# Scores of 64-wide heads as two float32r products over 128 rows, and weight loads issued ahead

## The chip, the cores and the metric

One core of one Trainium2 chip runs the whole program. The metric is device time in microseconds (us); of three executions of the kernel before, the median is 1943.73 us (1943.52 to 1948.55). Engines in the profile: PE is TensorE (matrix products), PEld its weight loads, DVE is VectorE, ACT is ScalarE, POOL is GpSimd, SP is SyncE, which here issues nearly all transfers.

## The reference

Two transformer blocks over 512 tokens of 1024 features in float32. The first has differential attention and a mixture of experts; the change leaves their work alone. The second has two layers, each a mixer and a convolution-gated feed-forward net. The even mixer has sparse attention, whose 128 keys per query are picked by a small index score, beside relative-position attention; the odd mixer has forgetting attention beside a sink-window attention. All their heads are 64 wide:

```python
qa, ka, va, qi, ki, wi, qb, kb, vb = _split(xn @ w_in, EVEN_SPLITS)
...
rel = jax.nn.relu(jnp.einsum('bqhd,bsd->bqhs', qib, k_idx).astype(jnp.float32))
score = jnp.einsum('bqhs,bqh->bqs', rel, wib)
_, idx = lax.top_k(score, topk)
...
logits = jnp.einsum('bqhd,bqkhd->bhqk', qb, k_sel).astype(jnp.float32) * scale            # sparse (dsa)
logits = jnp.einsum('bqhd,bshd->bhqs', qc, kc).astype(jnp.float32) * scale + bias[None]   # relative position (rel)
logits = (jnp.einsum('bqhd,bshd->bhqs', qb, k).astype(jnp.float32) * scale
          + fq[..., None] - f_cum[:, :, None, :])                                         # forgetting (forg)
logits = jnp.einsum('bnqkgd,bnskd->bnkgqs', qb, kband).astype(jnp.float32) * (dh ** -0.5) # window
p = jax.nn.softmax(logits, axis=-1).astype(v.dtype)
```

Each is masked before the softmax (the window's has a sink column beside it), and the probabilities multiply the values. `f_cum` is the cumulative log of the forget gates. Both halves of a mixer are joined and multiplied by `w_out`.

## The kernel before, in words

The residual lies feature-major (8 chunks of 128 features by 512 tokens). The program runs stage by stage; those of the change are C (even mixer, some 640 to 959 us of the profile) and E (odd mixer, some 1318 to 1565 us).

A big product is written as three products of type float32r, since a float32 number is held as a high and a low float32r part: high by high, high by low, low by high (`mm3`, L123 to L133). `load` (L114 to L118) brings raw weights into one of 3 buffers `wr`; `split` makes the high part `wh` by a cast on ACT (L110) and the low part `wl` by a subtraction on DVE (L111). `fm` makes feature-major outputs, 512 tokens wide; `tm` and `tm_cols` token-major ones.

A score is one plain float32 matmul of 64 contraction rows: block i of 128 queries against the first n = 128 (i + 1) keys, so n is 128, 256, 384 and 512 in each head (`soft_heads`, L641). There are three such sets of 8 heads: rel and dsa in C, forg in E. In forg a 65th row carries the decay: ones in `qa`, the sums in `ka` (`aug`). A score is followed by bias and minimum (L644, DVE), exponential (L645, ACT), reciprocal (L646) and scaling (L647, DVE), transposes (L656, PE), a copy (L658, ACT) and per head a group of value products (L668, PE). The index scores (L793) are 12 such products, with n of 256, 384 and 512; the window scores (L969) are 32, 8 of n = 128 and 24 of n = 256. Odd heads lie on partitions 64 to 127 of the `qk` tiles.

Work is emitted as units with a cost, and `weave` interleaves two lists of units at equal rates by those costs. The tile framework's list scheduler then fixes each engine's order. Each engine, and SP's queue, takes its instructions strictly in that order. Rope (`rot`, L370) sends four transfers of 64 KB each from a tile to the scratch tile `rsw`, all through SP's queue.

Of the kernel before, what the change touches and what calls it, by code (L numbers as in the profile page):

```python
# [4 lines left out]
F32 = mybir.dt.float32  # L5
# [11 lines left out]
BIG = 1e36  # L17
# [48 lines left out]
# per-feature vectors, packed as columns  # L66
# [15 lines left out]
class K:  # L82
# [3 lines left out]
    # ------------------------------------------------------------ helpers  # L86
# [14 lines left out]
    def split(self, raw, shape, eng=0, pool=None):  # L101
        """H, L with raw == H + L, both float32r"""
        nc = self.nc
        n = shape[1] * shape[2]
        pool, bufs = (pool, 2) if pool else (self.wp, self.nh)
        h = pool.tile([P, 1024], F32R, name="wh", tag="wh", bufs=bufs)
        l = pool.tile([P, 1024], F32R, name="wl", tag="wl", bufs=bufs)
        h = h[:, :n].rearrange("p (a b) -> p a b", a=shape[1])
        l = l[:, :n].rearrange("p (a b) -> p a b", a=shape[1])
        nc.scalar.copy(h, raw)  # L110
        (nc.gpsimd if eng else nc.vector).tensor_tensor(l, raw, h.bitcast(F32), op=OP.subtract)  # L111
        return h, l

    def load(self, src, k, n):  # L114
# [5 lines left out]
    def mm3(self, out, wh, wl, xh, xl, first, last, swap=False):  # L120
        """out += W^T x over the three products that carry float32"""
# [22 lines left out]
    # Work is emitted in units (cost, function). Units of several lists are woven, so that the tensor engine finds products to do  # L144
    # while the chain of a softmax or a norm is under way; what such a chain feeds to the tensor engine is put off by some units.
# [20 lines left out]
    def weave(a, b, tail=0):  # L166
        """one list, in which both go ahead at the same rate; the last units of b come after a"""
# [9 lines left out]
    def fm(self, w, x, done, sub=8):  # L177
        """feature-major product: done(m, psum[128 features, 512 tokens]); w [rows, cols]; x(k)->(H, L)"""
# [4 lines left out]
        raw, ps, hl = {}, {}, {}  # L183

        def unit(m, m0, per, k0, k1):
            def fn():
                if m == m0 and k0 == 0:
                    raw[0] = self.load(wv[:, :, m0 * P:(m0 + per) * P], nk, per * P)
# [14 lines left out]
        while m * P < cols:  # L203
            per = max(1, min(2048 // (nk * P), cols // P - m))
            for q in range(per):
# [6 lines left out]
    def tm(self, raws, n, x, done, nk=NK, fine=0):  # L212
        """token-major product: done(i, psum[128 tokens, n]); raws: list of (k0, k1, thunk of raw[P, k, n])"""
        ps, st, units = {}, {}, []

        def unit(k0, get, c0, c1, i):
            def fn():
                if c0 == k0 and i == 0:
                    st["raw"] = get()
# [13 lines left out]
        for k0, k1, get in raws:  # L233
            step = 1024 // n
            cuts = list(range(k0, k1, 1 if k0 < fine else step)) + [k1]
            for c0, c1 in zip(cuts, cuts[1:]):
                for i in range(NT):
                    units.append(((c1 - c0) * 3 * (n / 2400.0 + 0.003), unit(k0, get, c0, c1, i)))
# [14 lines left out]
    def sumsq(self, k):  # L253
        """self.acc: the squares of all chunks but the last; self.acc2: of the last"""
# [11 lines left out]
    def rsq(self, src, n, scale, eps=1e-6, name="rsq"):  # L266
        """(src * scale + eps) ** -0.5, [P, n]: a first guess by halving the exponent, then three steps of Newton's"""
# [33 lines left out]
    def norm_x(self, g):  # L301
        """k -> H, L of h*g, begun by the stage before or here"""
# [7 lines left out]
    def norm_lazy(self, g):  # L310
        """the same, but a chunk is made when it is first used, and the next ones with it"""
# [10 lines left out]
    def last_add(self, m, ps):  # L322
        """the last addition to a chunk of the residual in a stage"""
# [8 lines left out]
    def norm_r(self, want_b=True, now=False):  # L332
        """1 / root mean square: self.rt per token along the partitions, self.rb along the free axis"""
# [43 lines left out]
    # ------------------------------------------------------------ A: differential attention  # L377
    def stage_a(self):
# [3 lines left out]
        with tc.tile_pool(name="pa", bufs=1) as pa:  # L382
# [9 lines left out]
            # -lambda, on every partition  # L392
# [19 lines left out]
            # the queries are divided by the slopes of the heads, so that distances count 1 for all  # L412
# [157 lines left out]
    # ------------------------------------------------------------ conv gated ffn  # L570
# [57 lines left out]
    # ------------------------------------------------------------ 64-wide attention  # L628
    def soft_heads(self, pool, heads, begin):
        """units of causal attention over heads of 64; scores come negated. heads: list of dicts with q(i)->[K,128], k(n)->[K,n],  # L630
        bias(i, n)->[P,n], v(j)->[P,64], done(pv) for the second head of a pair"""
# [3 lines left out]
        def score(u, i):  # L635
# [5 lines left out]
            nc.tensor.matmul(s[:, :n], lhsT=hd["q"](i), rhs=hd["k"](n), start=True, stop=True)  # L641
# [7 lines left out]
        def turn(u, i):  # L649
# [7 lines left out]
            # block (key j, query i) lies at 3 j + i  # L657
# [17 lines left out]
        for t in range(len(us) + SOFT[1]):  # L675
            parts = [(f, us[t - d], c) for f, d, c in ((score, 0, 0.15), (turn, SOFT[0], 0.11), (value, SOFT[1], 0.3))
# [17 lines left out]
    # ------------------------------------------------------------ C: sparse + relative position attention  # L694
    def stage_c(self):
# [3 lines left out]
        self.nsb = 4  # L699
        with tc.tile_pool(name="pc", bufs=1) as pc:  # L700
            rc, rs = self.cst(pc, "ropec"), self.cst(pc, "ropes")
            tc_, ts_ = self.cst(pc, "tropec"), self.cst(pc, "tropes")
# [8 lines left out]
            def qk_tile(name, c0, n, scale, rope):  # L711
                def done(m, ps):
                    t = pc.tile([P, T], F32, name=name, tag="qk", bufs=10)
# [3 lines left out]
                    QK[name, m] = t  # L717
                return self.fm(w[:, c0:c0 + n], x, done)

            # va | ki | wi, 2 x 290 columns  # L720
# [22 lines left out]
            # layer norm and rope of the index keys, twice along the free axis so that both halves of the partitions get them  # L743
            k2 = pc.tile([P, NT, 2, 64], F32, name="k2")
            ki = pc.tile([P, T], F32, name="ki")
# [21 lines left out]
            def turn_keys():  # L767
# [3 lines left out]
                nc.scalar.copy(ki, tp)  # L771

# [3 lines left out]
            self.flush()  # L776

            # which keys each query keeps: bias 0 for kept, BIG for others
# [6 lines left out]
            def index_score(i, hh):  # L785
                def fn():
                    n = P * (i + 1)
                    if hh == 0:
                        scs[i] = pc.tile([P, T], F32, name="sc", tag="sc", bufs=2)
                    sc = scs[i]  # L790
                    b = slice(64 * (hh % 2), 64 * (hh % 2) + 64)
                    s = self.pst()
                    nc.tensor.matmul(s[:, :n], lhsT=QK["qi", hh // 2][b, i * P:(i + 1) * P], rhs=ki[b, :n], start=True,  # L793
                                     stop=True)
# [9 lines left out]
                return (0.3 * (i + 1), fn)  # L804
# [23 lines left out]
            self.emit(self.weave(index, qk_tile("qb", 1860, 512, -0.125, False) + qk_tile("kb", 2372, 512, 1.0, False)  # L828
                                 + self.tm_cols(w, 2884, 512, x, dvb)))
            yb, ya, mbs = [], [], {}  # L830

            def rel_bias(hh):
                def fn():
                    for q in range(hh + (hh > 0), min(8, hh + 2)):
                        make_bias(q)

# [9 lines left out]
            def head(kind, hh, v, begin, bias, y):  # L846
                c, b = hh // 2, slice(64 * (hh % 2), 64 * (hh % 2) + 64)
                return {"q": lambda i: QK["q" + kind, c][b, i * P:(i + 1) * P], "k": lambda n: QK["k" + kind, c][b, :n],
                        "bias": bias, "v": lambda j: v[:, j, hh * 64:hh * 64 + 64], "begin": begin, "done": self.y_out(y)}
# [5 lines left out]
            dsa = self.soft_heads(pc, [head("a", hh, va, lambda: None, lambda i, n: keep[:, ko[i]:ko[i] + n], ya)  # L855
# [4 lines left out]
    # ------------------------------------------------------------ E: forgetting attention + sink window  # L860
    def stage_e(self):
# [3 lines left out]
        self.nsb = 4  # L865
        with tc.tile_pool(name="pe", bufs=1) as pe:
            rc, rs = self.cst(pe, "ropec"), self.cst(pe, "ropes")
            wm, upto = self.cst(pe, "wmask"), self.cst(pe, "upto", tag="sb", bufs=self.nsb)
            # causal mask: 0 up to the diagonal, BIG beyond
# [9 lines left out]
            qa = pe.tile([65, 8, T], F32, name="qa")  # L879
            ka = pe.tile([65, 8, T], F32, name="ka")  # L880

            # vc | fc | vd, 2 x 324 columns; fc and the last of vc and vd come first
# [21 lines left out]
            def qk_tile(name, c0, n, scale):  # L904
                def done(m, ps):
                    t = pe.tile([P, T], F32, name=name, tag="qk", bufs=6)
                    nc.vector.scalar_tensor_tensor(t, ps, scale, self.rb, op0=OP.mult, op1=OP.mult)
                    self.rot(pe, t, t, rc, rs)
                    QD[name, m] = t
                    if name == "kd":  # L910
                        kx = QD["kx"] = pe.tile([P, T], F32, name="kx", tag="qk", bufs=6)

                        def cross():
                            nc.sync.dma_start(kx[0:64], t[64:128])
                            nc.sync.dma_start(kx[64:128], t[0:64])
                        self.after(4, cross)
                return self.fm(w[:, c0:c0 + n], x, done)

            def aug(dst, scale):
                def done(m, ps):  # L920
                    for e in range(2):
                        b = slice(64 * e, 64 * e + 64)
                        nc.vector.scalar_tensor_tensor(dst[0:64, 2 * m + e], ps[b], scale, self.rb[b], op0=OP.mult,
                                                       op1=OP.mult)
                return done
# [3 lines left out]
            # log forget gates, summed along the tokens: rows 64 of the keys  # L929
# [9 lines left out]
            def forget_sum():  # L939
# [4 lines left out]
                fr = pe.tile([8, T], F32, name="fr", tag="rsw", bufs=1)  # L944
# [685 lines left out]
```

## Time and profile before

| | us |
|---|---|
| median of three executions | 1943.73 |
| span of the profiled execution | 1942.3 |
| PE busy | 1884.1 (97%) |
| DVE busy | 1312.7 (68%) |
| ACT busy | 960.6 (49%) |
| PE's share of the chain of waits, float32 scores L641 | 3.2% |

The profiled execution is shown by its span, from the first to the last instruction; no other time of it is on the page. It lies 1.4 us below the median. Busy time is the union of an engine's instructions. The records of consecutive matmuls overlap, so the chain of waits, which gives each piece only what it adds to the end, is used for the cost of one, and not its mean duration. PEclk 1.00 is the 2.4 GHz level of TensorE's clock, 0.50 the 1.2 GHz level.

### The profile page before, as it was taken

To read this page: it belongs to the slowest core of one execution; us is meant where nothing else is said; L and a number is where in the kernel's file an instruction comes from. 1 tells how busy PE (TensorE), PEld (TensorE's weight loads), DVE (VectorE), ACT (ScalarE), POOL (GpSimd) and SP (SyncE) were. 2 spreads that over 40 slices of the span, in tenths; PEclk is the share of its full clock that TensorE was granted. 3 is DMA by queue.
4 is the path that set the end of the run, shared out by engine and by line. 5 is a ranking of instruction groups with operands and counts; after the bars stand their busy time and mean duration, and the time that the engine had idled before them with its cause. 6 is when DMAs were issued, how large, how long until landed. Compare 5 with 4: busy or idle time off the path is not lost.

```text
span 1942.3 us, 24143 instructions
## 1 busy us (share of the span) xinstructions
PE 1884.1 (97%) x8604; PEld 1452.6 (75%) x8605; DVE 1312.7 (68%) x2792; ACT 960.6 (49%) x1628; POOL 221.9 (11%) x274
## 2 busy tenths in 40 slices
PE   8999996999998899999999999999999999999997
PEld 6767585778886776665788888888666688888885
DVE  6586847999997697745577457744655577637753
ACT  5555645888885324345444234433445544324442
POOL 2000012322222202300100000012100110000001
PEclk9999997999999999999999999999999999999998
DMA  5522056999994422211232343234211133233231
GB/s 187 178 66 87 22 175 234 356 368 366 373 361 143 131 87 84 72 49 44 73 103 74 90 126 91 82 87 141 74 56 44 46 104 92 75 110 109 80 90 59
DMA packets 245680, 251.88 MB, mean 130 GB/s; under 512 B 11151, under 2 KB 172335, under 8 KB 245553
## 3 DMA queue, kind: packets, MB, share of 16 engines
q1 hardware_dynamic: 236272, 234.73, 37.9%
q0 software_dynamic: 5072, 10.00, 1.4%
q10 hardware_dynamic: 4208, 5.56, 0.8%
q8 instruction: 69, 1.13, 0.2%
q14 instruction: 59, 0.48, 0.1%
HBM read 238.19 MB, written 15.73 MB: 131 GB/s over the span
## 4 chain that ended last, share of the span: by engine, by line
PE 65%; DVE 2%; DMA 1%; issue 0%; ACT 0%; POOL 0%; DVEq 0%; ACTq 0%
PE mm L124 17%; PE mm L125 17%; PE mm L126 17%; PE s L641 3%; PE pv L668 3%; PE t L656 2%; PE mm L128 1%; PE mm L129 1%; PE mm L130 1%; PE s L969 1%; PE pv L1003 1%; DVE wl L111 1%; PE t L988 0%; PE s L793 0%; PE ss L338 0%
## 5 line engine op out<-in xcount | busy, mean ns | idle before, releaser
L110 ACT CAST wh<-wr 128x1024 fp32r<-128x1024 f32 (+5 forms) x335 | 306.7, 916 | 457.1 <-PE mm L125 329.0
L111 DVE TENSOR_TENSOR wl<-wr,wh 128x1024 fp32r<-128x1024 f32 (+4 forms) x332 | 353.6, 1069 | 214.4 <-ACT wh L110 211.7
L124 PE MATMUL mm<-xh,wh 128*128 128x512 f32 x952 | 374.3, 393 | 2.1 <-DVE h L365 1.8
L125 PE MATMUL mm<-xl,wh 128*128 128x512 f32 x952 | 372.3, 391 | 0.0
L126 PE MATMUL mm<-xh,wl 128*128 128x512 f32 x952 | 372.0, 391 | 0.0
L124 PEld LDWEIGHTS mm<-xh,wh 128*128 128x128 f32 x952 | 178.7, 188 | 45.7 <-issue 7.9
L126 PEld LDWEIGHTS mm<-xh,wl 128*128 128x128 f32 x952 | 178.8, 188 | 38.1 <-issue 1.4
L125 PEld LDWEIGHTS mm<-xl,wh 128*128 128x128 f32 x952 | 178.8, 188 | 37.4 <-issue 1.4
L111 DVE TENSOR_TENSOR wl<-wx,wh 128x1024 fp32r<-128x1024 f32 x123 | 151.6, 1250 | 12.4 <-ACT wh L110 5.8
L110 ACT CAST wh<-wx 128x1024 fp32r<-128x1024 f32 x134 | 139.5, 1050 | 28.1 <-PE mm L130 24.1
L128 PE MATMUL mm<-wh,xh 128*128 128x512 f32 (+2 forms) x352 | 132.7, 381 | 9.7 <-ACT wh L110 5.7
L125 PE MATMUL mm<-hl,wh 128*128 128x512 f32 x352 | 138.9, 395 | 0.0
L126 PE MATMUL mm<-hh,wl 128*128 128x512 f32 x352 | 138.9, 395 | 0.0
L124 PE MATMUL mm<-hh,wh 128*128 128x512 f32 x352 | 138.9, 395 | 0.0
L129 PE MATMUL mm<-wl,xh 128*128 128x512 f32 (+2 forms) x352 | 129.6, 368 | 1.4 <-DVE wl L111 1.4
L130 PE MATMUL mm<-wh,xl 128*128 128x512 f32 (+2 forms) x352 | 128.7, 366 | 0.0
L605 DVE TENSOR_TENSOR z<-mm,rb 128x512 f32<-128x512 f32 x88 | 60.3, 687 | 81.3 <-PE mm L126 81.3
L128 PE MATMUL mm<-wh,xeh 128*128 128x512 f32 x256 | 104.2, 407 | 0.8 <-ACT xeh L1262 0.8
L264 POOL TENSOR_TENSOR acc<-acc,sq 128x512 f32<-128x512 f32 x42 | 57.8, 1376 | 392.1 <-ACT sq L260 391.8
L130 PE MATMUL mm<-wh,xel 128*128 128x512 f32 x256 | 101.8, 397 | 0.0
L129 PE MATMUL mm<-wl,xeh 128*128 128x512 f32 x256 | 101.6, 397 | 0.0
L365 DVE TENSOR_TENSOR h<-mm,h 128x512 f32<-128x512 f32 x88 | 60.6, 690 | 58.3 <-PE mm L126 57.2
(386 smaller groups left out, 3324.7 us busy)
## 6 DMA issues: line engine op xcount, KB each, us to landing
wr<-in_ffn_w_up SPq DMA_DIRECT2D x88, 512.0 KB, 5.1
wx<-in_moe_w_gate SPq DMA_DIRECT2D x23, 1024.0 KB, 9.4
wx<-in_moe_w_up SPq DMA_DIRECT2D x22, 1024.0 KB, 9.0
wx<-in_moe_w_down SPq DMA_DIRECT2D x22, 1024.0 KB, 9.9
wr<-in_ffn_w_down SPq DMA_DIRECT2D x32, 704.0 KB, 4.5
wr<-in_da_w_in SPq DMA_DIRECT2D x11, 1024.0 KB, 5.1
wr<-in_even_w_in SPq DMA_DIRECT2D x11, 1024.0 KB, 5.3
wr<-in_moe_w_up SPq DMA_DIRECT2D x10, 1024.0 KB, 7.9
```

The source lines that it names most:

```text
L110: nc.scalar.copy(h, raw)
L111: (nc.gpsimd if eng else nc.vector).tensor_tensor(l, raw, h.bitcast(F32), op=OP.subtract)
L124: mm(out, lhsT=wh, rhs=xh, start=first, stop=False, skip_group_check=True)
L125: mm(out, lhsT=wh, rhs=xl, start=False, stop=False, skip_group_check=True)
L126: mm(out, lhsT=wl, rhs=xh, start=False, stop=last, skip_group_check=True)
L128: mm(out, lhsT=xh, rhs=wh, start=first, stop=False, skip_group_check=True)
L129: mm(out, lhsT=xh, rhs=wl, start=False, stop=False, skip_group_check=True)
L130: mm(out, lhsT=xl, rhs=wh, start=False, stop=last, skip_group_check=True)
L365: self.nc.vector.tensor_tensor(self.h[:, m], ps, self.h[:, m], op=OP.add)
L605: nc.vector.tensor_tensor(z[:, 2:], ps, self.rb, op=OP.mult)
L641: nc.tensor.matmul(s[:, :n], lhsT=hd["q"](i), rhs=hd["k"](n), start=True, stop=True)
L668: nc.tensor.matmul(pv[64 * e:64 * e + 64, j * P:], lhsT=heads[u]["v"](j), rhs=pt[:, 4 * j:3 * j + 4], start=j == 0, stop=j == NT - 1, skip ...
```

## The change

Scores. A query tile is cut into a high and a low float32r part (`nh` by ACT, `nl` by DVE). Transfers from SBUF to SBUF stack them for each head: `qs` holds high over low in 128 rows; `kh` holds the high part of the keys twice, `kl` their low part twice. Two float32r products over 128 rows are summed in PSUM: (high + low) queries with high keys, then with low keys. In forg the second product takes the tiles `q2` and `k2`, which also carry ones against the high and low rows of the decay.

```diff
+    def halves(self, pool, t):
+        nc = self.nc
+        h = pool.tile([P, T], F32R, name="nh", tag="nh", bufs=1)
+        l = pool.tile([P, T], F32R, name="nl", tag="nl", bufs=1)
+        nc.scalar.copy(h, t)
+        nc.vector.tensor_tensor(l, t, h.bitcast(F32), op=OP.subtract)
+        return h.bitcast(F32), l.bitcast(F32)
...
+    def q_stack(self, pool, t, tiles=None):
+        h, l = self.halves(pool, t)
+        out = []
+        for e in range(2):
+            s = tiles[e] if tiles else pool.tile([P, T], F32R, name="qs", tag="qs", bufs=self.nst)
+            self.nc.sync.dma_start(s.bitcast(F32)[self.half(e)], h[self.half(e)])
+            self.nc.sync.dma_start(s.bitcast(F32)[self.half(1 - e)], l[self.half(e)])
...
+    def k_stack(self, pool, t, low=None):
...
+            for n, name in enumerate(("kh", "kl")):
+                own = low is not None and n == 1
+                s = low[e] if own else pool.tile([P, T], F32R, name=name, tag=name, bufs=self.nst if n == 0 else self.nsl)
+                for to in (e,) if own else (e, 1 - e):
+                    self.nc.sync.dma_start(s.bitcast(F32)[self.half(to)], x[n][self.half(e)])
...
-            nc.tensor.matmul(s[:, :n], lhsT=hd["q"](i), rhs=hd["k"](n), start=True, stop=True)
+            for m, (q, k) in enumerate(hd["qk"](i, n)):
+                nc.tensor.matmul(s[:, :n], lhsT=q, rhs=k, start=m == 0, stop=m == 1)
```

Each such transfer moves 64 rows of 512, 128 KB. One pair of heads takes 12 of them in C (4 for the queries, 8 for the keys); in E a pair takes 12 and four of a single row. `prep` stacks the next pair when the scores of an odd head begin (C) or of an even one (E). The scratch `nh` is one buffer, and rope's `rsw` now uses the same; `nl` is one too. In C there are 18 such tiles to halve, in E 13. In E the 16 half-tile scalings of `aug` become 8 of whole tiles, and two cross transfers `kx` go.

```diff
+                more = lambda hh: lambda: prep("a", hh // 2 + 1) if hh % 2 and hh < 7 else None
...
-        sw = pool.tile([P, T], F32, name="rsw", tag="rsw", bufs=1)
+        sw = pool.tile([P, T], F32, name="rsw", tag="nh", bufs=1)
```

Loads. Each `fm` or `tm` registers its weight loads in the order in which they are needed, and the first use of one issues it and the next two:

```diff
+    def loaded(self, n):
+        while self.went < min(len(self.loads), n + 3):
+            self.raws[self.went] = self.loads[self.went]()
+            self.went += 1
+        return self.raws.pop(n)
```

The costs by which units are woven fall (a score's 0.15 to 0.11, an index score's 0.3 to 0.17, a window unit's 0.75 to 0.6), some buffer counts change, two rope tables share the buffers of `mb`, and the program's scratch for dynamic transfers is set to 8192.

Where instructions stand. First PE at the start of the dsa heads in C; `mm<-xh` is the last projection, `mm<-ybh` and `mm<-ybl` the output products of rel, `s` a score, `t` a transpose. Before:

```order
L128 MATMUL mm<-wh,xh_7155 128x290
L129 MATMUL mm<-wl,xh_7155 128x290
L130 MATMUL mm<-wh,xl_7157 128x290
L641 MATMUL s<-ka,qa 128x128
L641 MATMUL s<-ka,qa 128x256
L124 MATMUL mm<-ybh,wh 128x512
L125 MATMUL mm<-ybl,wh 128x512
L126 MATMUL mm<-ybh,wl 128x512
L641 MATMUL s<-ka,qa 128x384
L641 MATMUL s<-ka,qa 128x512
L124 MATMUL mm<-ybh,wh 128x512
L656 MATMUL t<-ident,sb 128x128
```

Now, at the end of 81 rows of output products (the first three of these are the last of them):

```order
L135 MATMUL mm<-ybh,wh 128x512
L136 MATMUL mm<-ybl,wh 128x512
L137 MATMUL mm<-ybh,wl 128x512
L694 MATMUL s<-kh,qs 128x128
L694 MATMUL s<-kh,qs 128x256
L135 MATMUL mm<-ybh,wh 128x512
L136 MATMUL mm<-ybl,wh 128x512
L137 MATMUL mm<-ybh,wl 128x512
L135 MATMUL mm<-ybh,wh 128x512
L136 MATMUL mm<-ybl,wh 128x512
L694 MATMUL s<-kl,qs 128x128
L694 MATMUL s<-kl,qs 128x256
```

Before, the first score follows the last projection directly and the output products stand between scores; now 81 of the 96 output products come ahead of the first score.

Second, PE at the border between two pairs of dsa heads (`pv` a value product). Before:

```order
L668 MATMUL pv<-ptall,va 64x512
L656 MATMUL t<-ident,sb 128x128 x2
L668 MATMUL pv<-ptall,va 64x384
L668 MATMUL pv<-ptall,va 64x256
L668 MATMUL pv<-ptall,va 64x128
L641 MATMUL s<-ka,qa 128x128
L656 MATMUL t<-ident,sb 128x128 x3
L641 MATMUL s<-ka,qa 128x256
L124 MATMUL mm<-ybh,wh 128x512
L656 MATMUL t<-ident,sb 128x128 x4
```

Now:

```order
L721 MATMUL pv<-ptall,va 64x128
L709 MATMUL t<-ident,sb 128x128 x4
L694 MATMUL s<-kh,qs 128x128
L694 MATMUL s<-kh,qs 128x256
L709 MATMUL t<-ident,sb 128x128 x3
L721 MATMUL pv<-ptall,va 64x512
L721 MATMUL pv<-ptall,va 64x384
L721 MATMUL pv<-ptall,va 64x256
L721 MATMUL pv<-ptall,va 64x128
L694 MATMUL s<-kl,qs 128x128
L694 MATMUL s<-kl,qs 128x256
```

The products with the high keys now stand ahead of the last values of the old pair, those with the low keys behind them, and the output product that stood there has moved.

Third, SP's queue at the same place in C. Before:

```order
L372 DMA rsw<-ka 32x512 x4
L839 DMA hk<-in_relext 128x512
L372 DMA rsw<-ka 32x512 x4
L117 DMA wr<-in_even_w_out 128x4x512
L372 DMA rsw<-ka 32x512 x8
L117 DMA wr<-in_even_w_out 128x4x512 x3
L592 DMA wr<-in_ffn_w_up 128x8x128 x22
```

Now:

```order
L128 DMA wr<-in_even_w_out 128x4x512
L385 DMA rsw<-ka 32x512 x8
L128 DMA wr<-in_even_w_out 128x4x512
L661 DMA qs<-nh 64x512
L662 DMA qs<-nl 64x512
L661 DMA qs<-nh 64x512
L662 DMA qs<-nl 64x512
L676 DMA kh<-nh 64x512 x2
L676 DMA kl<-nl 64x512 x2
L676 DMA kh<-nh 64x512 x2
L676 DMA kl<-nl 64x512 x2
```

The stacking transfers stand behind the last rope transfers and the weight loads, ahead of the first load of the feed-forward net. On all engines the order of the stages other than C and E is as before.

## Rows read from the trace of the kernel before

**Rows 1.** Page, part 1: busy us (share of the span) xinstructions.
```profile
PE 1884.1 (97%) x8604; PEld 1452.6 (75%) x8605; DVE 1312.7 (68%) x2792; ACT 960.6 (49%) x1628; POOL 221.9 (11%) x274
```

**Rows 2.** Busy time by stretch; columns: stretch, length, engines, PEclk, DMA share, GB/s.
```profile
668.00:741.00 73.00, 71.69 (x297) 53.58 (x296) 56.29 (x132) 19.18 (x26) 2.54 (x2) 1.00 0.29 90
741.00:854.00 113.00, 113.00 (x498) 73.69 (x496) 78.55 (x211) 47.74 (x117) 32.91 (x28) 1.00 0.27 79
854.00:921.00 67.00, 67.00 (x263) 36.60 (x262) 40.21 (x144) 37.15 (x106) 0.00 (x0) 1.00 0.10 31
1366.00:1469.00 103.00, 103.00 (x478) 72.01 (x477) 59.62 (x196) 49.90 (x172) 7.95 (x6) 1.00 0.20 62
1469.00:1526.00 57.00, 57.00 (x255) 36.45 (x254) 37.52 (x136) 34.05 (x99) 0.00 (x0) 1.00 0.06 19
```

**Rows 3.** Waits of PE from 668 to 921 us: total, times, longest.
```profile
PE s L793 <- DVE qi L375: 0.7, 1, 0.7
PE s L793 <- ACT rel L796: 0.6, 1, 0.6
```

**Rows 4.** Chain of waits by line: whole span, then 640 to 745 us.
```profile
by line: PE mm L124 16.9%; PE mm L125 16.6%; PE mm L126 16.6%; PE s L641 3.2%; PE pv L668 2.9%; PE t L656 1.7%; PE mm L128 1.3%; PE mm L129 1.3%; PE mm L130 1.3%; PE s L969 0.9%; PE pv L1003 0.7%; DVE wl L111 0.6%; PE t L988 0.4%; PE s L793
...
by line: PE mm L124 14.9%; PE mm L126 14.2%; PE mm L125 13.9%; PE mm L128 8.1%; PE s L793 7.8%; PE mm L130 7.4%; PE mm L129 7.3%; DMA wr<-in_even_w_in 4.9%; DVE wl L111 2.8%; PE s L641 2.6%; ACT wh L110 2.5%; issue 2.0%; PE ss L338 1.6%; DV
```

**Rows 5.** Chain, 741 to 752 us: start, length, what; heads of rel.
```profile
741.43 0.85 PE s L641 x4
742.27 0.43 PE mm L124
742.70 0.23 PE mm L125
...
743.17 1.98 PE s L641 x6
```

**Rows 6.** Chain, 858 to 866 us: heads of dsa.
```profile
858.16 0.41 PE s L641 x2
...
862.39 1.70 PE s L641 x4
```

**Rows 7.** Chain, 844 to 856 us: products 290 columns wide, then a value group.
```profile
849.29 0.13 PE mm L128
...
850.90 2.30 PE pv L668 x8
```

**Rows 8.** Lines on ACT and DVE, 640 to 960 us and 855 to 920 us, by shape.
```profile
L690 ACT CAST yah<-pv 128x512 fp32r<-128x512 f32 x4 | 2.3, 586 | 8.5 <-PE pv L668 8.5
...
L691 DVE TENSOR_TENSOR yal<-pv,yah 128x512 fp32r<-128x512 f32 x3 | 2.1, 686 | 1.9 <-ACT yah L690 1.9
```

**Rows 9.** DMA issues, 1318 to 1565 us: count, size, median us to landing.
```profile
kx<-kd SPq DMA_DIRECT2D x2, 128.0 KB, 2.3
```

**Rows 10.** Timeline of SP's queue: start, length, issue.
```profile
773.07 2.41 SPq L372 DMA_DIRECT2D rsw<-qa  x4
```

**Rows 11.** Busy time from 184 to 208 us, columns as in rows 2.
```profile
184.00:188.00 4.00, 3.53 (x23) 2.70 (x21) 0.95 (x5) 2.97 (x6) 0.00 (x0) 1.00 0.07 4
188.00:192.00 4.00, 2.76 (x14) 2.01 (x15) 3.96 (x34) 2.74 (x12) 0.00 (x0) 1.00 0.92 319
192.00:196.00 4.00, 4.00 (x15) 2.30 (x15) 3.53 (x20) 2.36 (x9) 0.00 (x0) 0.61 0.54 204
196.00:200.00 4.00, 4.00 (x9) 2.00 (x9) 1.58 (x10) 1.23 (x6) 0.00 (x0) 0.50 0.00 0
200.00:204.00 4.00, 4.00 (x13) 2.61 (x11) 1.50 (x7) 1.54 (x6) 0.00 (x0) 0.61 0.00 0
204.00:208.00 4.00, 3.90 (x22) 2.19 (x21) 3.39 (x19) 2.67 (x8) 0.00 (x0) 1.00 0.00 0
```

**Rows 12.** Waits of SP's queue, 640 to 960 us.
```profile
SPq L117 <- DVE wl L111: 95.3, 8, 28.2
```

More of the change, by code (lines that the diff above doesn't have):

```diff
@@ L112, in split, with ahead @@
         return h, l
+    def ahead(self, get):
+        self.loads.append(get)
+        return len(self.loads) - 1
+    def loaded(self, n):
[3 more added lines that the diff above has]
+        return self.raws.pop(n)
     def load(self, src, k, n):
@@ L182, in fm @@
         units = []
-        raw, ps, hl = {}, {}, {}
+        raw, ps, hl, turn = {}, {}, {}, {}
         def unit(m, m0, per, k0, k1):
@@ L187, in fn @@
                 if m == m0 and k0 == 0:
-                    raw[0] = self.load(wv[:, :, m0 * P:(m0 + per) * P], nk, per * P)
+                    raw[0] = self.loaded(turn[m0])
                 if k0 == 0:
@@ L204, in fm @@
             per = max(1, min(2048 // (nk * P), cols // P - m))
+            turn[m] = self.ahead(lambda m=m, per=per: self.load(wv[:, :, m * P:(m + per) * P], nk, per * P))
             for q in range(per):
@@ L214, in tm, with unit @@
         ps, st, units = {}, {}, []
-        def unit(k0, get, c0, c1, i):
+        def unit(k0, turn, c0, c1, i):
             def fn():
                 if c0 == k0 and i == 0:
-                    st["raw"] = get()
+                    st["raw"] = self.loaded(turn)
                 if i == 0:
@@ L233, in tm @@
         for k0, k1, get in raws:
+            turn = self.ahead(get)
             step = 1024 // n
@@ L237, in tm @@
                 for i in range(NT):
-                    units.append(((c1 - c0) * 3 * (n / 2400.0 + 0.003), unit(k0, get, c0, c1, i)))
+                    units.append(((c1 - c0) * 3 * (n / 2400.0 + 0.003), unit(k0, turn, c0, c1, i)))
         return units
@@ L626, in stage_ffn, with half @@
                 self.emit(self.fm(down[r0:r0 + HT * P], lambda k, hid=hid: hid[k], self.last_add if half else self.add_h))
+    def halves(self, pool, t):
[5 more added lines that the diff above has]
+        return h.bitcast(F32), l.bitcast(F32)
+    @staticmethod
+    def half(e):
+        return slice(64 * e, 64 * e + 64)
+    def q_stack(self, pool, t, tiles=None):
[5 more added lines that the diff above has]
+            self.nc.sync.dma_start(s.bitcast(F32)[self.half(1 - e)], l[self.half(e)])
+            out.append(s)
+        return out, h
+    def k_stack(self, pool, t, low=None):
+        x = self.halves(pool, t)
+        out = []
+        for e in range(2):
+            both = []
+            for n, name in enumerate(("kh", "kl")):
[3 more added lines that the diff above has]
+                    self.nc.sync.dma_start(s.bitcast(F32)[self.half(to)], x[n][self.half(e)])
+                both.append(s)
+            out.append(both)
+        return out
     def soft_heads(self, pool, heads, begin):
@@ L675, in soft_heads @@
         for t in range(len(us) + SOFT[1]):
-            parts = [(f, us[t - d], c) for f, d, c in ((score, 0, 0.15), (turn, SOFT[0], 0.11), (value, SOFT[1], 0.3))
+            parts = [(f, us[t - d], c) for f, d, c in ((score, 0, 0.11), (turn, SOFT[0], 0.11), (value, SOFT[1], 0.3))
                      if 0 <= t - d < len(us)]
@@ L712, in done @@
                 def done(m, ps):
-                    t = pc.tile([P, T], F32, name=name, tag="qk", bufs=10)
+                    t = pc.tile([P, T], F32, name=name, tag="qk", bufs=8)
                     nc.vector.scalar_tensor_tensor(t, ps, scale, self.rb, op0=OP.mult, op1=OP.mult)
@@ L717, in done, with prep @@
                     QK[name, m] = t
+                    if (name, m) == ("kb", 0):
+                        self.after(2, lambda: prep("b", 0))
                 return self.fm(w[:, c0:c0 + n], x, done)
+            stacks = {}
+            def prep(kind, c):
+                q, _ = self.q_stack(pc, QK.pop(("q" + kind, c)))
+                k = self.k_stack(pc, QK.pop(("k" + kind, c)))
+                for e in range(2):
+                    stacks[kind, 2 * c + e] = q[e], *k[e]
             def va_raw(part, k):
@@ L776, in stage_c @@
             self.flush()
+            qis = [pc.tile([P, 2, T], F32R, name="qis", tag="ptall", bufs=2) for _ in range(2)]
+            for c in range(2):
+                self.q_stack(pc, QK.pop(("qi", c)), [qis[c][:, e] for e in range(2)])
             keep = pc.tile([P, 1280], F32, name="keep")
@@ L790, in fn @@
                     sc = scs[i]
-                    b = slice(64 * (hh % 2), 64 * (hh % 2) + 64)
                     s = self.pst()
-                    nc.tensor.matmul(s[:, :n], lhsT=QK["qi", hh // 2][b, i * P:(i + 1) * P], rhs=ki[b, :n], start=True,
-                                     stop=True)
+                    q = qis[hh // 2][:, hh % 2, i * P:(i + 1) * P]
+                    for m, k in enumerate((kih, kil)):
+                        nc.tensor.matmul(s[:, :n], lhsT=q, rhs=k[:, :n], start=m == 0, stop=m == 1)
                     r = pc.tile([P, T], F32, name="rel", tag="sb", bufs=self.nsb)
@@ L854, in stage_c @@
                                                  + qk_tile("ka", 512, 512, 1.0, True)) + va_units(0, d0)))
-            dsa = self.soft_heads(pc, [head("a", hh, va, lambda: None, lambda i, n: keep[:, ko[i]:ko[i] + n], ya)
+            more = lambda hh: lambda: prep("a", hh // 2 + 1) if hh % 2 and hh < 7 else None
+            dsa = self.soft_heads(pc, [head("a", hh, va, more(hh), lambda i, n: keep[:, ko[i]:ko[i] + n], ya)
                                        for hh in range(8)], lambda: ya.extend([self.x8("yah"), self.x8("yal")]))
@@ L878, in stage_e @@
             fz = pe.tile([P, NT, 8], F32, name="fz")
-            qa = pe.tile([65, 8, T], F32, name="qa")
-            ka = pe.tile([65, 8, T], F32, name="ka")
+            q2 = [pe.tile([P, T], F32R, name=f"q2{n}") for n in range(4)]
+            k2 = [pe.tile([P, T], F32R, name=f"k2{n}") for n in range(4)]
+            for n in range(4):
+                o = self.half(1 - n % 2)
+                nc.gpsimd.memset(q2[n].bitcast(F32)[o], 1.0)
+                nc.gpsimd.memset(k2[n].bitcast(F32)[o], 0.0)
+            stacks = {}
             def v_raw(part, k):
@@ L905, in done, with prep @@
                 def done(m, ps):
-                    t = pe.tile([P, T], F32, name=name, tag="qk", bufs=6)
+                    t = pe.tile([P, T], F32, name=name, tag="qk", bufs=8)
                     nc.vector.scalar_tensor_tensor(t, ps, scale, self.rb, op0=OP.mult, op1=OP.mult)
-                    self.rot(pe, t, t, rc, rs)
                     QD[name, m] = t
[L910 to L916, printed above, removed]
-                return self.fm(w[:, c0:c0 + n], x, done)
[L919 to L925, printed above, removed]
+                    if name[1] == "d":
+                        self.rot(pe, t, t, rc, rs)
+                    if (name, m) == ("kc", 0):
+                        self.after(2, lambda: prep(0))
+                return self.fm(w[:, c0:c0 + n], x, done)
+            def prep(c):
+                n = 2 * (c % 2)
+                q, h = self.q_stack(pe, QD.pop(("qc", c)))
+                for e in range(2):
+                    nc.sync.dma_start(q2[n + e].bitcast(F32)[self.half(e)], h[self.half(e)])
+                k = self.k_stack(pe, QD.pop(("kc", c)), k2[n:n + 2])
+                for e in range(2):
+                    o = self.half(1 - e).start
+                    for r, f in enumerate((fh, fl)):
+                        nc.sync.dma_start(k2[n + e].bitcast(F32)[o + r:o + r + 1], f.bitcast(F32)[2 * c + e:2 * c + e + 1])
+                    stacks[2 * c + e] = (q[e], k[e][0]), (q2[n + e], k2[n + e])
             v_units = lambda part, d: self.tm([(k, k + 4, (lambda k=k: v_raw(part, k))) for k in (0, 4)], 324, x, d)
+            fhl = pe.tile([40, T], F32R, name="fhl")
+            fh, fl = fhl[0:8], fhl[32:40]
             def forget():
@@ L968, in w_score @@
                 s = self.pst()
-                nc.tensor.matmul(s[:, :n], lhsT=QD["qd", c][b, i * P:(i + 1) * P], rhs=kt[b, lo:lo + n], start=True,
-                                 stop=True)
+                for m, k in enumerate(kds[hh // 4]):
+                    nc.tensor.matmul(s[:, :n], lhsT=qds[hh][:, i * P:(i + 1) * P], rhs=k[:, lo:lo + n], start=m == 0,
+                                     stop=m == 1)
                 sb = sbs[hh, i] = pe.tile([P, 256], F32, name="sbw", tag="sb", bufs=self.nsb)
@@ L1015, in fn @@
                         f(*u)
-                window.append((0.75, fn))
-            self.emit(self.weave(window, self.fm(w[:, 0:512], x, aug(qa, -0.125)) + self.fm(w[:, 512:1024], x, aug(ka, 1.0))
-                                 + v_units(0, d0)))
-            heads = [{"q": lambda i, hh=hh: qa[:, hh, i * P:(i + 1) * P], "k": lambda n, hh=hh: ka[:, hh, :n],
+                window.append((0.6, fn))
+            proj = qk_tile("qc", 0, 512, -0.125) + qk_tile("kc", 512, 512, 1.0) + v_units(0, d0)
+            self.emit(proj[:2])
+            self.emit(self.weave(window, proj[2:]))
+            heads = [{"qk": lambda i, n, hh=hh: [(q[:, i * P:(i + 1) * P], k[:, :n]) for q, k in stacks[hh]],
                       "bias": lambda i, n: cm[:, T - n:T], "v": lambda j, hh=hh: vc[:, j, hh * 64:hh * 64 + 64],
-                      "begin": lambda: None, "done": self.y_out(yc)} for hh in range(8)]
+                      "begin": lambda hh=hh: prep(hh // 2 + 1) if hh % 2 == 0 and hh < 6 else None,
+                      "done": self.y_out(yc)} for hh in range(8)]
             forg = self.soft_heads(pe, heads, lambda: yc.extend([self.x8("ych"), self.x8("ycl")]))
@@ L1524, in run @@
         self.later, self.nx = [], None
+        self.loads, self.raws, self.went = [], {}, 0
         self.moe = "ab" in stages
```

49 lines of the change are left out of this document (30 added, 19 removed).

## The prediction

> **What bounds the kernel now.** Three views were read in this order. First the page's busy times: PE is busy for 97% of the span [rows 1], so what shortens PE's own work shortens the kernel, as long as PE stays fed. Second the busy time by stretch, since an average hides stages: in the five stretches that hold the scores, PE is busy for all of the time in four and for 71.69 of 73 us in the fifth [rows 2]. DVE has 56.29 of 73 us in the index stretch, 78.55 of 113 in that of the rel heads, 40.21 of 67 in dsa, and less than two thirds in the window and forg stretches: there is room, least where the index scores stand. Third PE's waits: 0.7 and 0.6 us in the 253 us from the index scores to the end of dsa [rows 3]. So PE is the bound at each place that the change touches, and no softmax chain or load stands ahead of it there.
>
> What the old scores cost is read from the chain of waits by line [rows 4]: L641 has 3.2% of 1942.3 us, or 62 us; L969 0.9%, or 17.5 us; L793 7.8% of the 105 us from 640 to 745, or 8.2 us. Together 88 us. The pieces bear this out: scores of 128 and 256 columns took 0.85 us together [rows 5], of 384 and 512 took 1.70 us [rows 6], so a head has 2.55 us, and 24 heads 61.
>
> **What the scores become.** A float32r product of 512 columns takes 0.23 us on the chain [rows 5], one of 290 columns 0.13 [rows 7]. On the line between these two, 384 columns take 0.17, and 256 columns, a little outside, 0.12. Nothing in the trace shows a float32r product of 128 columns; I take 0.12 for it too, which is dear, as half of the 290 would be 0.06. A head is then 2 x (0.12 + 0.12 + 0.17 + 0.23) = 1.28 us, and 24 heads 31. A window head is 2 x 4 x 0.12 = 0.96, and eight are 7.7. An index head is 2 x (0.12 + 0.17 + 0.23) = 1.04, and four are 4.2. That is 43 us in place of 88: minus 45.
>
> Two smaller terms I set against each other. The first float32r product after a float32 score takes 0.43 us where the next takes 0.23 [rows 5], so some 40 such exits lose 8 us that the new scores need not lose. On the other hand the transposes and value products beside the scores are still float32, so the new scores have entries and exits of their own; at half of 0.20 for some 80 of them that is 8 us as well. Without the second the gain would be 53. From the other side, a narrow product could run at float32's pace. Scores of 896 columns took 1.70 us [rows 6] and of 384 columns 0.85 [rows 5], so 128 columns stream in 0.21 at that pace; each of the 64 new products of that width would cost 0.21 instead of 0.12, 6 us in all, of which I take half, 3 us. If the 256-column ones did so too, that is a rival below.
>
> The Trainium skill has a rule that speaks against the change: its page "TensorEngine Tiling (Array Packing)", section When to Use Tiling, holds that contractions of 64 rows or fewer should run as two row tiles at once, so that a 64-row score is not wasteful by itself and a 128-row one gives the second tile away. By that rule two heads' old scores would cost one. The trace has a hint and no more: three scores, the last from the pair's other head, took 1.98 us [rows 5], where the pieces 1.70 and 0.41 [rows 6] give 2.11. So 0.13 us of overlap is in the 88 us already, and the rule takes nothing further from the gain, since the kernel before did not pair its scores.
>
> **What the halving and stacking cost.** Each of 31 tiles takes a cast on ACT of 0.59 us and a subtraction on DVE of 0.69 [rows 8], 18 and 21 us in all, on engines that have room [rows 2]. A transfer of 64 rows of 512, as the new ones are, 128 KB, lands 2.3 us after its issue [rows 9], and four issues hold SP's queue for 2.41 us [rows 10], 0.60 each. Twelve are 7.2 us of SP per pair. The sharpest place is the border between two pairs of dsa heads. Counted from the start of the odd head: the cast of the queries ends at 0.6, their subtraction at 1.3; the third issue starts at 1.9 and lands at 4.2, and only then is the one buffer `nh` free for the keys; the cast of the keys ends at 4.8, the fourth issue lands at 4.8 and frees `nl`, so the subtraction ends at 5.5; two issues of `kh` and two of `kl` start from 4.8 on, the last at 6.6, and it lands at 8.9. The border comes one head of PE work later: scores 1.3 and their entries 0.3, transposes 1.4 (1.7% of the span over 24 heads, rows 4), values 2.30 [rows 7]: 5.3 us. So 3.6 us are missing at each of three borders, 11 us. Before, the output products lay between the scores there; now 81 of 96 are spent ahead of the first dsa head, and the 15 that are left are 3.5 us. I let half of these help and take 9 us, with 0 and 18 as ends (other work covers it; ACT and DVE take each step late, behind softmax work).
>
> Queued behind a `kl` score that waits are, on PE, transposes and values of the old pair and all that follows; ACT and DVE wait for those in turn. So a stall here also drains the softmax line.
>
> Index and rel: the first index score now stands 71 products behind the key transposes, not 10, so 61 x 0.23 = 14 us later, while DVE's 56.29 us of that stretch [rows 2] grow by about ten subtractions, 7 us. DVE and PE then end nearly together. I take 6 us for C outside dsa, ends 0 and 15. In E the next pair is stacked two heads ahead, 10.6 us against 8.9 plus four more issues, 2.4: nearly level. I take 3 us, ends 0 and 8.
>
> Clock: between 184 and 192 us PE was busy for 3.53 and 2.76 of 4 us, and the granted clock then stood at 0.61, 0.50 and 0.61 for three slices of 4 us, PE being busy throughout, before it was back at 1.00 [rows 11]. That cost (0.39 + 0.50 + 0.39) x 4 = 5.1 us. In all five stretches of the scores it is now 1.00 [rows 2]. Stalls of about 3 us might bring such a fall; I take 3 us, rather more than half of one, ends 0 and 12.
>
> **Loads ahead and the rest.** PE waits for no load in the stretches of rows 3, and outside C and E the order on SP is as before, so I give the earlier issue nothing. SP's queue waited 95.3 us for weight buffers in C [rows 12], longest 28.2, with nothing urgent behind; now transfers stand behind such loads, but at the dsa heads the loads ahead of them take buffers whose splits are done early. The halved scalings of `aug` are DVE time that hides.
>
> **The sum.** Minus 45, plus 3 (narrow), 9 (dsa), 6 (rest of C), 3 (E), 3 (clock): minus 21. From the span of 1942.3 that is 1921.3; the median lies 1.4 above the span, so 1923 us.
>
> **Rivals.** *All of it is kept*: the waits are covered and the gain is 45, 1899 us. For it: PE never waits now, and 15 output products remain for three borders. Against: PE has less work to hide the same softmax chains. *Waits eat it*: the upper ends of dsa and C with 6 for E and 3 for the clock, 42 in all, 1941 us. For it: one `nh` buffer, which makes the keys wait for the queries' transfers. Against: the rel heads have projections between them.
> *Slower by the clock*: stalls at the twelve borders (three each in rel, dsa, window and forg) bring the 1.2 GHz level each time. A fall costs 5.1 us; with 21 us of other losses it decides from six falls on (minus 45 plus 21 plus 31), and eight give plus 17, 1960 us. For it: rows 11. Against: the one fall followed two slices with idle time, and other short gaps of C [rows 3] left the clock at 1.00. *Slower by narrow products*: those of 128 and 256 columns run at the float32 pace. That gives back 6 us for the first and, at (0.43 - 0.12) x 104 products (256 columns stream in twice 0.21), 32 us for the second, so the scores gain 7 us, the other terms cost 21, and the time is 1958 us. For it: the narrowest float32r product in the trace has 290 columns, and 84 of the 140 scores are narrower. Against: at 290 columns the pace is still that of 512.
>
> **How the numbers follow.** Chances: forecast 0.50 (1908 to 1936 by its terms), all kept 0.17, eaten 0.17, clock 0.08, narrow 0.08. Measurement tells 0.3%, 5.8 us, from no change. Faster takes the first two and 0.05 of the third, 0.72; within 0.3% gets 0.09 of the third and 0.02 of the slow cases, 0.11; slower the rest, 0.17. The range runs from 1897, a little below all kept, to 1946, which takes in the eaten case and leaves out most of the two slow ones.
>
> **What would show it.** In the profile after: a 512-column half of a score at 0.23 us and a 128-column one at 0.12 or less on the chain; the chain's share of scores down from 88 to 43 to 55 us; PE waits of 3 us or so at three dsa borders, with `s` waiting for transfers of `kl`; PEclk of 1.00 in C and E. The prediction is wrong if narrow products take over 0.2 us, if PE's waits in C and E sum to under 5 or over 40 us, or if stages other than C and E change their length by more than 2 us.

## The result, and the profile after

The changed kernel takes 1922.9 us (median of four executions, 1915.89 to 1925.08), the kernel before in the same runs 1946.0 (1943.52 to 1948.55). The ratio is 0.9879, with a 95% interval of 0.9854 to 0.9905: faster by 1.2%, clear of 0.3%. The forecast was 1923.

First part 1 of the page of the changed kernel, which answers to [rows 1]:

```profile
PE 1841.3 (96%) x8604; PEld 1451.1 (76%) x8605; DVE 1321.3 (69%) x2817; ACT 975.1 (51%) x1660; POOL 227.3 (12%) x281
```

The span is 1919.5 us. PE is busy for 42.8 us less than before and idle for 78.2 us instead of 58.2: PE's work fell by 43 us and idle time took 20 back. The first `ss` products of the stages (the sums of squares of the norms) give the stages' lengths: C goes from 319.0 to 310.3 us, E from 241.5 to 225.2, the two feed-forward nets stay within 0.1 us, and what lies ahead of C is 1.8 us longer, where the order is the same.

Busy time by stretch, columns as in rows 2: index, rel with the output products behind it, dsa, the end of C, window, forg.

```profile
684.00:737.00 53.00, 53.00 (x238) 43.56 (x237) 48.46 (x119) 17.47 (x27) 0.00 (x0) 1.00 0.51 144
737.00:864.00 127.00, 119.49 (x580) 88.53 (x578) 97.14 (x242) 55.67 (x132) 34.15 (x28) 1.00 0.45 122
864.00:916.00 52.00, 45.83 (x211) 27.85 (x210) 32.29 (x130) 32.63 (x96) 0.00 (x0) 1.00 0.50 122
916.00:952.00 36.00, 32.03 (x134) 22.21 (x134) 21.39 (x38) 20.18 (x37) 10.09 (x11) 1.00 0.30 84
1388.00:1442.00 54.00, 53.40 (x293) 39.61 (x294) 41.18 (x175) 41.41 (x159) 0.00 (x0) 1.00 0.47 121
1452.00:1510.00 58.00, 58.00 (x284) 39.21 (x284) 41.71 (x150) 39.79 (x112) 0.00 (x0) 1.00 0.39 96
```

PE has no idle time in the index and forg stretches and 0.6 us in the window's; in rel, dsa and the end of C it misses 7.5, 6.2 and 4.0 us. PEclk is 1.00 in all six. What PE waited for (total, times, longest), first in rel, then from 864 us to the end of C; smaller rows are left out. [rows 3], which ends with dsa, has no wait in rel or dsa:

```profile
PE s L694 <- DVE st L697: 3.1, 3, 2.3
PE t L709 <- DVE sb L700: 2.6, 3, 1.1
```

```profile
PE t L709 <- ACT ptall L711: 4.3, 9, 0.7
PE pv L721 <- ACT ptall L711: 2.2, 4, 0.7
...
PE t L709 <- DMA kl<-nl: 0.6, 1, 0.6
```

In rel PE waits for the softmax steps on DVE. In dsa the transfers of `kl` cost 0.6 us once. The rest is short waits, 13 of them for the copy of transposes on ACT. Nine hold up transposes: there is one PSUM tile `t`, as before, so a block can't be turned until the one before it is copied out, and PE has nothing else to do meanwhile. Four hold up value products, which read the copy.

What the new scores cost, from the chain of waits in forg (as rows 5 to 7):

```profile
1454.71 0.17 PE s L694 x2
...
1457.41 0.36 PE s L694 x2
...
1458.00 0.47 PE s L694 x2
...
1501.71 0.24 PE s L694 x2
```

Each piece is one score, its two products: 128, 384, 512 and 256 columns.

### The profile page after: what moved, and what is told of

It reads as the page before. It is cut to its first block, busy times and chain, and to the rows that moved or that the text cites. A ratio compares the mean times of both kernels' runs of the same rounds, so it can differ in the third digit from the quotient of the medians.

```text
span 1919.5 us, 24632 instructions
## 1 busy us (share of the span) xinstructions
PE 1841.3 (96%) x8604; PEld 1451.1 (76%) x8605; DVE 1321.3 (69%) x2817; ACT 975.1 (51%) x1660; POOL 227.3 (12%) x281
## 3 DMA queue, kind: packets, MB, share of 16 engines
q8 instruction: 69, 1.13, 0.2%
## 4 chain that ended last, share of the span: by engine, by line
PE 56%; DVE 7%; DMA 2%; ACT 2%; issue 1%; POOL 1%; SPq 0%; DVEq 0%; ACTq 0%; POOLq 0%
PE mm L135 15%; PE mm L137 15%; PE mm L136 15%; PE pv L721 2%; PE t L709 1%; DVE wl L111 1%; DVE sc L884 1%; DVE m L883 1%; PE mm L139 1%; PE mm L140 1%; PE mm L141 1%; PE s L694 1%; PE pv L1095 1%; DVE sb L697 1%; ACT sb L698 0%
```

## The experiments

**The loads alone.** The kernel before with `ahead` and `loaded` and no other edit:

```diff
+            turn[m] = self.ahead(lambda m=m, per=per: self.load(wv[:, :, m * P:(m + per) * P], nk, per * P))
-                    raw[0] = self.load(wv[:, :, m0 * P:(m0 + per) * P], nk, per * P)
+                    raw[0] = self.loaded(turn[m0])
```

> The kernel before with nothing but the weight loads issued up to three early. Theory (nothing waits for a load where the order could change): 0 to 1 us against the kernel before, the same order of products in C and E, PE's waits unchanged. Rival (part of the 23 us comes from the loads): 4 us or more faster, with the waits of PE for wh and wl shorter.

Measured: ratio 1.0002 (0.9988 to 1.0015), 1945.2 against 1944.43 us. The loads alone give nothing, so the gain comes with the stacked scores. Apart from them two things were not tried: the loads beside the stacks, and the smaller weaving costs, which go with the stacks in every run that has them.

**The stacks in E alone, and in C alone.** The changed kernel, with the other stage's function taken from the kernel before (the first pair of lines is C's, for stacks in E alone, the second E's):

```diff
-                return {"qk": qk, "bias": bias, ...
+                return {"qk": lambda i, n: [(QK["q" + kind, c][b, i * P:(i + 1) * P], QK["k" + kind, c][b, :n])], ...
...
-            heads = [{"qk": lambda i, n, hh=hh: [(q[:, i * P:(i + 1) * P], k[:, :n]) for q, k in stacks[hh]], ...
+            heads = [{"qk": lambda i, n, hh=hh: [(qa[:, hh, i * P:(i + 1) * P], ka[:, hh, :n])], ...
```

> The changed kernel with the old 64-row float32 scores in C, so stacked scores in E alone. By the trace of the changed kernel E is 16 us shorter: 16 us faster than the kernel before, ratio about 0.992, the two sets adding up to the whole change. Rival (C and E help each other through the loads): less than 12 us, or a sum with the other half that misses 23 us by over 5.

Measured: 0.9924 (0.9903 to 0.9945), 1930.46 us; E is 226.0 us long.

> The changed kernel with the old float32 scores and augmented tiles in E, so stacked scores in C alone. By the trace C is 9 us shorter, of 25 us by which its scores are cheaper: 9 us faster than the kernel before, ratio about 0.9955, with some 17 us of waits of PE in C. Rival (waits in C are an accident of one execution): 15 us or more faster.

Measured: 0.9971 (0.9958 to 0.9985), 1939.04 us; C is 309.8 us long, and PE's waits are there again, 4.6 us in 10 for the copy `ptall` ahead of transposes. The two halves are worth 15 and 6 us (0.76% and 0.29% of 1944.43), 20 together against 23. They add up within the intervals. The 9 us expected of C lie just outside its interval; the stage itself is 9 us shorter in both traces (309.8 and 310.3 against 319.0). By either figure C, with 25 of the 45 us by which scores should be cheaper, gives a good deal less than E.

**Rope's scratch by itself.**

```diff
-        sw = pool.tile([P, T], F32, name="rsw", tag="nh", bufs=1)
+        sw = pool.tile([P, T], F32, name="rsw", tag="rsw", bufs=1)
```

> The changed kernel with one edit: rope's scratch has a buffer of its own again and does not share that of the high halves. Theory 1 (the shared buffer holds the first dsa stack behind the last ropes, so that 81 output products are spent ahead of the dsa heads and transposes then wait for the copy of the ones before with nothing between): no output product stands ahead of the first dsa head, PE's waits in dsa go from about 10 us to under 3, and the time falls by 7 to 10 us to about 1914. Theory 2 (the prediction's: the transfers of kl are late at the borders, since one buffer holds the high halves of queries and keys): waits for kl of about 3 us at three borders stay, and the time changes by less than 3 us.

Measured: 1896.2 us, ratio to before 0.9750 (0.9728 to 0.9772): against the changed kernel's 0.9879 that is 1.3% more, some 25 us, over twice what theory 1 gave; theory 2 is out. C is 286.3 us long, not 310.3, E 222.7, not 225.2. No output product stands ahead of the dsa heads. Its page, part 1, and then the stretches of rel, of dsa and of the end of C:

```profile
PE 1834.4 (97%) x8604; PEld 1453.1 (77%) x8605; DVE 1321.5 (70%) x2817; ACT 974.8 (51%) x1660; POOL 225.4 (12%) x281
```

```profile
736.00:838.00 102.00, 99.02 (x499) 73.08 (x498) 84.91 (x221) 51.17 (x125) 33.16 (x28) 1.00 0.56 149
838.00:890.00 52.00, 52.00 (x259) 35.51 (x258) 39.08 (x140) 36.07 (x104) 0.00 (x0) 1.00 0.44 107
890.00:929.00 39.00, 38.12 (x168) 28.67 (x167) 23.38 (x40) 20.92 (x36) 9.62 (x11) 1.00 0.37 103
```

The dsa heads take 52 us as before the edit, but PE has 259 matmul records there in place of 211 and is busy throughout. The 81 output products (18.6 us at 0.23) that stood ahead of dsa now fill it and the end of C. Why they stood ahead: in the changed kernel the first tile of dsa is halved only when the last rope has left the shared buffer. The rope's addition on DVE and the cast behind it on ACT, and then the same cast with rope's own buffer:

```profile
853.76 0.69 DVE L388 TENSOR_TENSOR ka<-ka,rsw 128x512 f32<-128x512 f32 x1 [1.19 <-POOL ka L387]
```

```profile
854.48 0.62 ACT L648 CAST nh<-qa 128x512 fp32r<-128x512 f32 x1
```

```profile
803.30 0.62 ACT L648 CAST nh<-qa 128x512 fp32r<-128x512 f32 x1 [0.68 <-DMA kh<-nh]
```

The cast moves from 10 us ahead of the first dsa score (864 us) to 35 us ahead of it (838 us). The parts of C, from the first score of one set to the first of the next, with the 81 products counted at dsa:

| us | before | changed | own scratch |
|---|---|---|---|
| start of C to the first rel score | 101.3 | 95.3 | 93.3 |
| rel | 112.8 | 108.3 | 101.7 |
| dsa and the end of C | 105.0 | 106.7 | 91.4 |

So the changed kernel spent more time than the one before from dsa on, although its scores there are 10 us cheaper; of the 24 us that the edit gave back, 15 lie there, 7 in rel and 2 ahead of it.

Theory 1 had priced the waits alone. PE's idle time falls by 18.2 us (78.2 to 60.0) and its busy time by another 6.9 (1841.3 to 1834.4). Counted from the start of each PE instruction to the start of the next, idle time left out, scores take 27.0 us in C of the changed kernel and 23.0 here, transposes 20.2 and 16.2. The same instructions cost more where fewer other products stand between them; that this is the reason was not tried by itself.

**One shared buffer, or sharing at all.**

```diff
-        h = pool.tile([P, T], F32R, name="nh", tag="nh", bufs=1)
+        h = pool.tile([P, T], F32R, name="nh", tag="nh", bufs=2)
...
-        sw = pool.tile([P, T], F32, name="rsw", tag="nh", bufs=1)
+        sw = pool.tile([P, T], F32, name="rsw", tag="nh", bufs=2)
```

> The changed kernel with rope's scratch and the high halves still under one name, but with two buffers. Theory 1 (a single shared buffer holds the dsa stacks behind the ropes): 20 us or more faster than the changed kernel, 1895 to 1903, no output product ahead of the dsa heads. Rival (it is the sharing as such, each halving still waiting its turn behind a rope): less than 10 us faster, 1913 or more.

Measured: 1896.78 us, 0.9757 (0.9739 to 0.9774), no product ahead of dsa. A second buffer under the same name does as well as a buffer apart, within the intervals: it was the single buffer. (In its one trace C is 290.1 us long, against 286.3.)

**The step at the borders.**

```diff
+        sw = pool.tile([P, T], F32, name="rsw", tag="rsw", bufs=1)
...
+        h = pool.tile([P, T], F32R, name="nh", tag="nh", bufs=2)
```

> Rope's own scratch, and two buffers for the high halves (the projection tiles have 7 buffers, not 8, to make room). The prediction's step at the borders (the keys' cast waits for the queries' transfers, 3.6 us at each of three dsa borders): 6 to 10 us faster than with the own scratch alone, 1886 to 1890. Rival (the output products between the heads cover it): within 2 us of 1896.

Measured: 1894.5 us, 0.9741 (0.9726 to 0.9756), within 2 us of rope's scratch alone; C is 287.5 us against 286.3. That the keys' cast waits for the queries' transfers costs nothing that can be measured. This version and the one with the own scratch alone beat both kernels, by 2.6% and 2.5%.

**No stacks made.**

```diff
     def q_stack(self, pool, t, tiles=None):
...
+        return [t, t], t
...
     def k_stack(self, pool, t, low=None):
...
+        return [[t, t], [t, t]]
```

> The changed kernel without the making of the stacks: no halves, no stacking transfers; both products of a score read the projection tiles of the pair as they are, 128 rows (so the scores are other sums), and those tiles have 12 and 10 buffers. Theory 1 (the stacks are hidden but for the scratch shared with rope): within 4 us of the version with rope's own scratch, 1892 to 1900. Theory 2 (making the stacks costs by itself, through DVE, ACT and the queue): 1888 or less.

Measured: 1891.59 us, 0.9734 (0.9715 to 0.9752), just under the line of theory 1 and above that of theory 2. In the profiles C is 287.3 us and E 222.6, as with the stacks made (286.3 and 222.7); the difference lies ahead of C (638.4 against 643.1 us), where nothing was edited and the ten traces range from 635.8 to 644.6. So 31 casts and subtractions and all the stacking transfers cost nothing that can be measured in C and E once the buffer is free.

**Two heads in turn.** In the kernel before, for dsa:

```diff
+            us = [(u + e, i) for u in range(0, len(heads), 2) for i in range(NT) for e in range(2)]
```

> The kernel before with one edit: in dsa the two heads of a pair take turns, so that scores of equal width on rows 0 to 63 and 64 to 127 follow each other. If such scores run side by side, the 20 us of the dsa scores shrink by 6 to 10 us and two scores of 512 columns take little over one's time on the chain. If they run one after the other, the time stays within 3 us of before, and two of 512 columns take about twice 0.85 us.

Measured: 0.9994 (0.9984 to 1.0005), 1943.76 us: the time stays. But the chain of waits at the first pair reads:

```profile
855.45 0.42 PE s L641 x4
...
857.01 0.63 PE s L641 x4
```

Each score is two instructions, so four are two scores, one of each head. Two of 128 columns together took 0.42 us, where one alone took 0.41 [rows 6]; two of 256 together 0.63, and one alone, in dsa of the kernel before:

```profile
861.18 0.63 PE s L641 x2
```

Two of 512 columns stand next to each other as well. PE's timeline (start, length) there, and then of one alone in the kernel before:

```profile
862.05 1.13 PE L641 MATMUL s<-ka,qa 64*128 64x512 f32 x4
```

```profile
873.10 1.12 PE L641 MATMUL s<-ka,qa 64*128 64x512 f32 x2
```

They run side by side. The first two of 384 columns stand apart, a transpose between them, and each costs its own 0.84; another two of 512, at 917 us, start 0.36 us apart and take 1.42 on the chain. C is 316.7 us long, against 319.0 before and 318.3 in the run with the loads alone; a difference of that size is not shown by one trace each. The scheduler left few equal scores next to each other: of 16 possible pairs four stand so. What a kernel with all of them adjacent would take stays open.

## Why the prediction was right, point by point

The total was met by luck: errors on either side cancelled. With waits out of the way (rope's own scratch) PE is busy for 49.7 us less than before (1884.1 to 1834.4); the changed kernel has 6.9 us more of busy time than that and 20.0 more idle than before. Minus 49.7 plus 6.9 plus 20.0 is minus 22.8, the change of the span. The forecast had minus 45 and plus 24 in their place.

- **The price of the new scores** was right: 0.17, 0.24, 0.36 and 0.47 us sum to 1.24 a head, against 1.28. The 128-column product takes half of 0.17, less than the 0.12 that I took, so the 3 us for narrow products were not due, and the rival of narrow products is out.
- **Entries and exits against each other** was mis-sized. I set 8 us of exits against 8 us of new entries and got 45; with rope's own scratch PE's work in C and E falls by 52.7 us, at the other end that I kept, 53. Counted from the start of one instruction to the start of the next, idle time left out, scores fall by 39.3 us (87.2 to 47.9, where I had 43, which leaves some 5 for the new entries) and the products by 6.8, near the 8 of exits. The transposes fall by 6.9 (36.8 to 29.9), for which the sum had no term.
- **The waits** had nearly the right size, 20.0 us of idle time against 18, and the wrong cause. I gave 9 us to the borders of dsa, since `kl` lands 8.9 us after the stack is begun, and 6 to the rest of C. The step that failed is the border's, "only then is the one buffer `nh` free for the keys": the keys do wait there, but the borders cost 0.6 us by `kl` and not 3.6 at each of three, and beside rope's own scratch a second buffer for the halves changes nothing. What held the stacks was the other user of that buffer, rope. I had the 81 output products in front of me and priced only the cover they took from the borders, not the whole dsa stretch that runs without filler, nor rel, where the same buffer is in the way. Idle and busy time together, that is about 25 us of span (1919.5 to 1894.4).
- **All kept** (1899 us, 0.17) is what the design gives with one buffer more; the argument against it, less work to hide the same softmax chains, did not hold: in dsa PE is then busy for all of 52 us.
- **E** was right in size: the two sums are 20 gross, 16.3 kept where I had 17, and 2.5 of the rest come back with rope's own scratch.
- **The clock** stayed at 1.00 in the six stretches of C and E above, so 3 us were not due and the rival is out; waits as short as those above, 2.3 us at most, brought no fall.
- **The loads** at nothing was right, and shown by itself.
- **Row tiles.** The Trainium skill's rule, "TensorEngine Tiling (Array Packing)", section When to Use Tiling, that contractions of 64 rows can run two at a time, agrees with this case's trace where two scores are adjacent: 0.42 us for two. My 0.13 us of overlap undersold it, but the conclusion stands, since the kernel before didn't set such scores side by side. Whether pairing all the old scores would have gained as much as stacking them was not tried.

## What to carry to other kernels

When a new tile takes the name of an old scratch to save space, ask what the old user is still doing when the new one is first needed; here one buffer of 2 KB a partition was worth 1.3%, more than the 1.2% that the change kept without it. Work that a scheduler pulls ahead is no gain where PE is always busy: look for what it was to fill. And a total that comes out right says little on its terms until each has been taken away by itself.

## What the runs showed of the hardware that was not expected

Two float32 scores of 64 rows on the two halves of the partitions cost what one costs when they stand next to each other and start together (0.42 and 0.63 us, and 1.13 against 1.12, above). And a transfer from SBUF to SBUF took three times as long as usual behind a weight load. In the changed kernel, SP's queue and then the chain of waits:

```profile
783.88 0.54 SPq L789 DMA_DIRECT2D wr<-in_even_w_in  x1
784.51 1.25 SPq L662 DMA_DIRECT2D qs<-nl  x2
```

```profile
785.17 7.02 DMA qs<-nl
```

One transfer of a stack, 128 KB, took 7.02 us there; the median of the sixteen `qs<-nl` in C is 2.3. That it was the load was not tried by itself.
